# The last group of each feed-forward stage multiplied block by block instead of as seven products

## The chip, the cores and the metric

The kernel is one program on one core of a Trainium2 chip. The metric is device time in microseconds (us) of one execution; the profile shows one such execution in detail. TensorE is called PE (its weight loads PEld), VectorE DVE, ScalarE ACT, GpSimd POOL and SyncE SP.

## The reference

Two transformer-like blocks are applied to 512 tokens of width 1024, in float32: a first block (a convolution branch, two attentions, a merge, then a feed-forward stage) and a second one (attention, feed-forward, state-space layer, feed-forward). Only the three feed-forward stages matter here:

```python
# first block
h2 = rms_norm(x, g_mlp[l])
x = x + jnp.square(jax.nn.relu(h2 @ w_up[l])) @ w_down[l]      # 1024 -> 4096 -> 1024

# second block, after the attention (layer 0) and after the state-space layer (layer 1)
def conv_ffn(h, w_in, conv_w, conv_b, w_out):                  # 1024 -> 2 x 2816, 2816 -> 1024
    gate, up = jnp.split(h @ w_in, [D_FF_2], axis=-1)
    gate = causal_dwconv(gate, conv_w, conv_b)
    return (jax.nn.silu(gate) * up) @ w_out
```

The three stages come in this order: that of the first block, followed by the attention of the second block; `conv_ffn` layer 0, followed by the state-space layer; `conv_ffn` layer 1, after which the output is written.

## The kernel before

Activations and weights are split into a high part (float32 rounded to fp32r) and a low part (the remainder), and every product is three matmuls: high by high, high by low, low by high. ACT makes the high part by a cast, DVE the low part by a subtraction (`whi`, `wlo` for weights; `hh`/`hl`, `mhh`/`mhl`, `ffh`/`ffl`, `fsh`/`fsl` for features). All matmuls of a weight matrix are 128x128 by 128x512.

The whole kernel is a list of jobs, run one after the other by `run_jobs`. A job is a piece of a weight matrix; while one job's matmuls are issued, ACT and DVE split the weights of the next ones, up to nine chunks of 128x512 ahead, and generators (`spawn`) work on the results of earlier jobs. Which instruction stands before which on an engine is settled when the program is written, by a running estimate of each engine's time.

- `jobA` multiplies features by 256 columns of weights, features kept on the partitions of the result (banks `ga`). `jobB` and `projB` keep tokens on the partitions (banks `gb`): for each of four token tiles of 128 tokens they multiply by 512 columns. `projB` cuts the contraction into jobs of a few 128-row pieces (four, unless `cut` says otherwise) and holds four banks open between them. Their weights are loaded by SP into the two `raw` buffers, the next job's load being issued when the first chunk of this job is split.
- `Feat` holds split features: `put` casts and subtracts one 128x512 piece as soon as it is there, `rd` waits for it.
- `residual(half)` adds a bank to the residual stream `x` (two halves of 512 columns, four token tiles) and then calls `x_done`, which starts the sum of squares (`junk`), the transposes (`tr`) and the split of that piece for the next stage.

A feed-forward stage goes through its hidden features in groups: four of 1024 in the first block; 1024, 1024 and 768 in `conv_ffn`. A group's way down to 1024 columns is `seven`: its hidden features (512 tokens by 8 or 6 pieces of 128) and its rows of the weight matrix are each cut into 2 by 2 blocks, and the eight block products are replaced by seven products of sums of blocks (banks `gw`). The weight blocks are loaded by SP into the buffers `b` (`get`) and added up by POOL with accumulating DMAs (`add`). The hidden features stay whole in a `Hidden` object (`ffr`, `fsr`), and `operands` makes the left factor of each of the seven, in the order of the table SEVEN, each at most one product ahead of the one that PE is at (NOP): `11` and `12` are plain blocks, `s1`, `s4`, `s2`, `s3` are sums (in the profile `ffs`, `fss`, with `wt` between), `22` is a block again. After each product two pieces of `x` are updated by DVE.

The products of a group stand between the jobs of the next group's way up. The last group has no next group: its seven products stand alone, one behind the other, and `LASTS` says after which of them a piece of `x` is complete.

Of the kernel before, what the change touches and what calls it, by code (L numbers as in the profile page):

```python
# [21 lines left out]
KD = 8  # L22
# [49 lines left out]
def kernel(ctx: ExitStack, tc: tile.TileContext, ins: dict, out: bass.AP, parts=(1, 2, 3, 4, 5)):  # L72
# [481 lines left out]
    LASTS = {1: (0, 1), 4: (0, 0), 5: (1, 0), 6: (1, 1)}  # L554
    NOP = 2

# [75 lines left out]
    def seven(wap, r0, nk, H, scale, last, pre=None):  # L632
# [23 lines left out]
        def product(i):  # L656
            name, bk, new, (row, half, sign), over = SEVEN[i]

            def run(wt):
                quota[0] = 4  # L660
                if new:
                    for t in range(2):
                        banks[bk, t] = bank("g", "gw")
                order = [(k, t) for k in range(hk) for t in range(2)]
                by_token = last and i == 6
                if by_token:
                    order = [(k, t) for t in range(2) for k in range(hk)]

                def evac(t):
                    tt = 2 * row + t  # L670
                    xa = x_half(tt, half)
                    if over:
                        hand_over()
                    dve.scalar_tensor_tensor(out=xa, in0=banks[bk, t], scalar=scale(sign)[:, tt:tt + 1], in1=xa,
                                             op0=ALU.mult, op1=ALU.add)
                    if over:
                        rel("t")
                    if last and LASTS.get(i) == (row, half):
                        x_done(tt, half)

                for n, (k, t) in enumerate(order):
                    wh, wl = wt.get(k, 0, 512)
                    h, l = (x[:, t * 128:(t + 1) * 128] for x in H().at(name, k))
                    ps = banks[bk, t]
                    s, e = bool(new) and k == 0, k == hk - 1
                    pe.matmul(ps, lhsT=h, rhs=wh, start=s, stop=False, skip_group_check=True)
                    pe.matmul(ps, lhsT=h, rhs=wl, start=False, stop=False, skip_group_check=True)
                    pe.matmul(ps, lhsT=l, rhs=wh, start=False, stop=e, skip_group_check=True)
                    if by_token and e:
                        evac(t)  # L690
                    if n % 2 and n + 1 < len(order):
                        if not by_token:
                            wt.done()
                        yield
                H().done += 1
                if not by_token:
                    for t in range(2):
                        evac(t)
                yield

            return run
# [4 lines left out]
        for i in range(7):  # L706
            j = Job(None, hk, 512, product(i), pre if i == 0 else None)
            j.speed = 1.2
            j.source = lambda c, i=i: R[src[i]][:, c * 512:(c + 1) * 512]
            j.after = after[i]  # L710
            if i == 0:
                j.ahead = lambda: get("0", 1, 1)
                j.prefetch = lambda i: (get("2", 2, 1), get("1", 2, 2))
            out.append(j)
# [122 lines left out]
    def residual(c, last=True):  # L837

        def evac(tt, ps):
            xa = x_half(tt, c)  # L840
            dve.tensor_add(xa, ps, xa)
            if last:
                x_done(tt, c)
        return evac
# [4 lines left out]
    def first_block():  # L849
# [422 lines left out]
        def up_evac(g, k0):  # L1272
            def evac(ft, ps):
                if k0 + ft == 0:
                    F[g] = Hidden("ff", KD)
                F[g].half((k0 + ft) // 4)
# [3 lines left out]
                def rest():  # L1280
                    act.activation(out=F[g].slot(k0 + ft), in_=r, func=AF.Square)
                    F[g].got.add(("r", k0 + ft))
                    yield
# [8 lines left out]
        def down(g):  # L1292
            return seven(ins["w_down"], g * 1024, KD, lambda: F[g], lambda sign: G["by token"](sign, 2), g == 3,
                         (lambda: hooks.update(x=hooks["next1"])) if g == 3 else None)
# [3 lines left out]
        for g in range(4):  # L1298
            p = down(g)
            jobs.append(p[0])  # L1300
            if g == 3:
                jobs.extend(p[1:])
                break
            for i, ps in enumerate((p[1:3], p[3:5], p[5:7], ())):
                up(g + 1, i, (lambda g=g: F[g + 1].work()) if i == 3 else None)
                jobs.extend(ps)

# [211 lines left out]
    def conv_ffn(layer, G, nxt):  # L1519
# [17 lines left out]
        def up_evac(k0, g, base):  # L1537
            def evac(ft, ps):
                k = k0 + ft
                if k == base:  # L1540
                    F[g] = Hidden("fs", groups[g][1])
                until(lambda: k in gt)
                y = gt.pop(k)
                dve.tensor_mul(F[g].slot(k - base), ps, y)
                F[g].got.add(("r", k - base))
            return evac

        def down(g, base, nk, last):
            return seven(wo, base * 128, nk, lambda: F[g], lambda sign: G["by token"](sign, 1), last,
                         (lambda: hooks.update(x=hooks[nxt])) if last else None)  # L1550
# [4 lines left out]
        for g, (base, n) in enumerate(groups):  # L1555
            if p:
                jobs.append(p.pop(0))
            for i in range(n // 2):
# [4 lines left out]
                     pre=(lambda g=g: F[g].work()) if i == n // 2 - 1 else None)  # L1563
# [3 lines left out]
            p = down(g, base, n, g == 2)  # L1567
        jobs.extend(p)
# [424 lines left out]
```

## Time and profile before

| | |
|---|---|
| median of the runs | 2552.32 us (lowest 2549.96 us) |
| the profiled execution, its own time | 2547.46 us |
| its span in the trace | 2545.7 us |
| PE busy, PE weight loads busy | 97%, 78% of the span |
| DVE, ACT, POOL busy | 65%, 45%, 11% |
| TensorE clock granted, mean | 0.991 of full speed |

The span runs from the first to the last instruction of the profiled execution; its own time has 1.8 us around that. Matmuls overlap each other in the records (each is drawn 0.39 us long though the next starts 0.23 us later), so the distance from one start to the next is what a matmul costs.

### The profile page before, as it was taken

The numbers are of one execution on the slowest core, as the hardware profiler recorded it, in microseconds if no ns is written. First come the engines' busy times: TensorE is split into PE (matmuls) and PEld (weight loads), VectorE is DVE, ScalarE is ACT, GpSimd is POOL, SyncE is SP. The second block draws the span as 40 slices with busy tenths as digits, with TensorE's granted clock in tenths as the row PEclk, the third lists the DMA queues.
The fourth block names the chain that finished last, engine by engine and source line by source line (L and its number), as shares of the span: only waits on it lengthen the run. The fifth ranks groups of instructions, "written<-read, shape, count | busy, mean of one in ns | idle before, by whom it ended". The sixth has DMA issues, their size and how long they took to land.

```text
span 2545.7 us, 30879 instructions
## 1 busy us (share of the span) xinstructions
PE 2460.7 (97%) x11496; PEld 1977.5 (78%) x11496; DVE 1660.3 (65%) x3041; ACT 1154.7 (45%) x2451; POOL 290.4 (11%) x328
## 2 busy tenths in 40 slices
PE   8999999999999999989898999998999998999997
PEld 6777777788888888867676888885778886888886
DVE  6435679953444566676877566677688686667676
ACT  6445565632234444544555333334466535434333
POOL 1000111201110101122210000001011011001011
PEclk9999999999999999999999999999999998999999
DMA  5212222233233556642121354554333431245454
GB/s 203 100 66 89 94 67 68 68 126 103 90 135 114 131 137 156 149 83 85 34 100 34 113 136 116 132 122 83 107 96 89 120 112 58 89 143 116 133 112 107
DMA packets 213110, 268.45 MB, mean 105 GB/s; under 512 B 6976, under 2 KB 149696, under 8 KB 212960
## 3 DMA queue, kind: packets, MB, share of 16 engines
q1 hardware_dynamic: 189200, 220.21, 26.4%
q0 software_dynamic: 20736, 39.85, 9.8%
q10 hardware_dynamic: 3024, 6.42, 0.7%
q8 instruction: 90, 1.47, 0.2%
q14 instruction: 60, 0.49, 0.1%
HBM read 262.20 MB, written 4.26 MB: 105 GB/s over the span
## 4 chain that ended last, share of the span: by engine, by line
PE 87%; DVE 8%; ACT 1%; issue 1%; DMA 1%; POOL 1%; SPq 0%; ACTq 0%; DVEq 0%; POOLq 0%
PE ga L87 48%; PE gb L87 17%; PE gw L87 13%; PE y L87 2%; PE z L87 1%; DVE wlo L120 1%; PE as L87 1%; PE o L87 1%; PE aT L92 1%; DVE ae L120 1%; DVE x L120 1%; PE tr L92 1%; DVE sm L120 1%; DVE fy L120 1%; PE xs L87 1%
## 5 line engine op out<-in xcount | busy, mean ns | idle before, releaser
L87 PE MATMUL ga<-hh,whi 128*128 128x512 f32 x1672 | 668.9, 400 | 0.9 <-ACT hh L120 0.9
L87 PE MATMUL ga<-hh,wlo 128*128 128x512 f32 x1672 | 653.5, 391 | 0.3
L87 PE MATMUL ga<-hl,whi 128*128 128x512 f32 x1672 | 652.6, 390 | 1.0 <-DVE hl L120 1.0
L120 DVE TENSOR_TENSOR wlo<-raw,whi 128x512 fp32r<-128x512 f32 x661 | 454.8, 709 | 225.9 <-ACT whi L120 225.4
L120 ACT CAST whi<-raw 128x512 fp32r<-128x512 f32 x661 | 389.8, 616 | 134.8 <-PE ga L87 75.8
L87 PEld LDWEIGHTS ga<-hh,whi 128*128 128x128 f32 x1672 | 314.4, 188 | 70.1 <-issue 4.4
L87 PEld LDWEIGHTS ga<-hl,whi 128*128 128x128 f32 x1672 | 314.6, 188 | 68.0 <-issue 2.2
L87 PEld LDWEIGHTS ga<-hh,wlo 128*128 128x128 f32 x1672 | 314.0, 188 | 68.6 <-DVE wlo L120 1.1
L120 DVE TENSOR_TENSOR wlo<-b,whi 128x512 fp32r<-128x512 f32 x266 | 177.7, 685 | 40.9 <-ACT whi L120 40.6
L120 ACT CAST whi<-b 128x512 fp32r<-128x512 f32 x266 | 156.2, 616 | 60.1 <-DMA b<-in_ffn_w_out_dram 30.8
L87 PE MATMUL gb<-whi,hh 128*128 128x512 f32 (+1 forms) x416 | 169.9, 408 | 0.2 <-ACT hh L120 0.2
L120 DVE SCALAR_TENSOR_TENSOR x<-gw,rsp,x 128x512 f32<-128x512 f32 x140 | 100.2, 750 | 105.9 <-PE gw L87 105.7
L87 PE MATMUL gb<-whi,hl 128*128 128x512 f32 (+1 forms) x416 | 160.3, 385 | 1.3 <-DVE asc L120 1.3
L87 PE MATMUL gb<-wlo,hh 128*128 128x512 f32 (+1 forms) x416 | 159.7, 384 | 0.9 <-DVE wlo L120 0.9
L120 ACT ACTIVATE fy<-fy,cols 128x512 f32<-128x512 f32 x60 | 43.5, 725 | 211.5 <-DVE fy L120 211.5
L87 PE MATMUL gw<-whi,fss 128*128 128x512 f32 x352 | 115.9, 401 | 15.2 <-DVE fss L120 9.0
L652 POOL DMA_DIRECT2D b<-in_ffn_w_out_dram x48 | 55.5, 1238 | 610.6 <-DVE wlo L120 523.9
L120 DVE SCALAR_TENSOR_TENSOR fy<-fg,cols,fy 128x510 f32<-128x510 f32 (+1 forms) x136 | 102.8, 756 | 4.8
L120 DVE TENSOR_TENSOR fg<-ga,R 128x512 f32<-128x512 f32 x68 | 46.8, 689 | 82.4 <-PE ga L87 69.8
L87 PEld LDWEIGHTS gw<-whi,fss 128*128 128x128 f32 x352 | 66.9, 192 | 34.2 <-DVE fss L120 12.5
L87 PEld LDWEIGHTS gb<-whi,hl 128*128 128x128 f32 x416 | 78.9, 190 | 17.5 <-DVE hl L120 1.6
L87 PE MATMUL gw<-whi,ffs 128*128 128x512 f32 x256 | 83.0, 398 | 9.2 <-DVE ffs L120 7.9
(296 smaller groups left out, 4072.9 us busy)
## 6 DMA issues: line engine op xcount, KB each, us to landing
raw<-in_ffn_w_in_dram SPq DMA_DIRECT2D x44, 1024.0 KB, 5.1
raw<-in_w_in_dram SPq DMA_DIRECT2D x40, 1024.0 KB, 5.0
b<-in_ffn_w_out_dram POOLq DMA_DIRECT2D x40, 512.0 KB, 5.7
raw<-in_w_up_dram SPq DMA_DIRECT2D x16, 1024.0 KB, 5.4
b<-in_w_down_dram POOLq DMA_DIRECT2D x32, 512.0 KB, 6.0
raw<-in_ssm_w_in_dram SPq DMA_DIRECT2D x16, 1024.0 KB, 5.2
b<-in_w_down_dram SPq DMA_DIRECT2D x12, 1024.0 KB, 7.8
b<-in_ffn_w_out_dram SPq DMA_DIRECT2D x12, 1024.0 KB, 7.9
```

The lines of the kernel that those rows point to most:

```text
L87: nc.tensor.matmul(o, lhsT=lhsT, rhs=rhs, **kw)
L92: nc.tensor.transpose(o, i, idn)
L120: return fn(*args, **kw)
L652: nc.gpsimd.dma_start(out=r3(R[nm][:, a * 512:(c + 1) * 512], c + 1 - a), in_=dram(i, j, a, c + 1), accum_op=ALU.add)
```

## The change

`seven` loses the arguments for a last group; it now runs for all groups but the last. The last group's features go into a `Feat`, split piece by piece as they come, and its way down is two `projB` calls, one for each half of the 1024 columns: eight pieces of contraction in jobs of four and four in the first block, six pieces in jobs of two and four (`cut=[2, 4]`) in `conv_ffn`. `residual` takes a per-token scale and then does the update of `x` with `scaled_add`, the same instruction that `seven` uses. The last group has 1024 hidden features in the first block and 768 in `conv_ffn`.

```diff
-    LASTS = {1: (0, 1), 4: (0, 0), 5: (1, 0), 6: (1, 1)}
     NOP = 2
+
+    def scaled_add(ps, scale, tt, half):
+
+        xa = x_half(tt, half)
+        dve.scalar_tensor_tensor(out=xa, in0=ps, scalar=scale[:, tt:tt + 1], in1=xa, op0=ALU.mult, op1=ALU.add)
...
-    def seven(wap, r0, nk, H, scale, last, pre=None):
+    def seven(wap, r0, nk, H, scale):
...
-    def residual(c, last=True):
+    def residual(c, last=True, scale=None):
 
         def evac(tt, ps):
             xa = x_half(tt, c)
-            dve.tensor_add(xa, ps, xa)
+            if scale:
+                scaled_add(ps, scale(), tt, c)
+            else:
+                dve.tensor_add(xa, ps, xa)
             if last:
                 x_done(tt, c)
...
                 if k0 + ft == 0:
-                    F[g] = Hidden("ff", KD)
-                F[g].half((k0 + ft) // 4)
+                    F[g] = Hidden("ff", KD) if g < 3 else Feat("ff", KD)
+                if g < 3:
+                    F[g].half((k0 + ft) // 4)
...
                 def rest():
+                    if g == 3:
+                        act.activation(out=r, in_=r, func=AF.Square)
+                        yield from F[g].put(k0 + ft, r)
+                        return
...
-        for g in range(4):
+        for g in range(3):
             p = down(g)
             jobs.append(p[0])
-            if g == 3:
-                jobs.extend(p[1:])
-                break
             for i, ps in enumerate((p[1:3], p[3:5], p[5:7], ())):
-                up(g + 1, i, (lambda g=g: F[g + 1].work()) if i == 3 else None)
+                up(g + 1, i, (lambda g=g: F[g + 1].work()) if i == 3 and g < 2 else None)
                 jobs.extend(ps)
+        for half in range(2):
+            projB(ins["w_down"], 3 * 1024, KD, half * 512, lambda: F[3],
+                  residual(half, True, lambda: G["by token"](1, 2)),
+                  pre=(lambda: hooks.update(x=hooks["next1"])) if half == 0 else None)
...
-                    F[g] = Hidden("fs", groups[g][1])
+                    F[g] = Hidden("fs", 8) if g < 2 else Feat("fs", 8)
                 until(lambda: k in gt)
                 y = gt.pop(k)
+                if g == 2:
+                    dve.tensor_mul(y, ps, y)
+                    spawn(F[g].put(k - base, y), 0.9)
+                    return
...
-            p = down(g, base, n, g == 2)
-        jobs.extend(p)
+            p = []
+            if g < 2:
+                p = seven(wo, base * 128, n, lambda g=g: F[g], lambda sign: G["by token"](sign, 1))
+        for half in range(2):
+            projB(wo, 16 * 128, 6, half * 512, lambda: F[2], residual(half, True, lambda: G["by token"](1, 1)),
+                  cut=[2, 4], pre=(lambda: hooks.update(x=hooks[nxt])) if half == 0 else None)
```

Three places in the order of the instructions. On PE in the last group of the first block, as it was before, where the product `s1` begins (`gw` a bank, `ff` and `ffs` left factors of the seven, `x` a piece of the residual stream that is transposed into `tr`):

```order
L87 MATMUL gw<-whi_3_9217,ff_9147 128x512
L87 MATMUL gw<-whi_0_9230,ffs_9233 128x512
L87 MATMUL gw<-wlo_0_9231,ffs_9233 128x512
L87 MATMUL gw<-whi_0_9230,ffs_9233 128x512 x2
L87 MATMUL gw<-wlo_0_9231,ffs_9233 128x512
L87 MATMUL gw<-whi_0_9230,ffs_9233 128x512
L92 MATMUL tr<-ident,x_6506 128x128 x8
```

The same engine now, at the beginning of the last group, where the way up (`ga`) ends:

```order
L87 MATMUL ga<-hh_6805,wlo_3_9099 128x512
L87 MATMUL gb<-whi_0_9112,ffh_8631 128x512
L87 MATMUL gb<-wlo_0_9113,ffh_8631 128x512
L87 MATMUL gb<-whi_0_9112,ffl_8632 128x512
L87 MATMUL gb<-whi_1_9123,ffh_8631 128x512
L87 MATMUL gb<-wlo_1_9124,ffh_8631 128x512
L87 MATMUL gb<-whi_1_9123,ffl_8632 128x512
```

Before, each product of a sum needed a left factor made since the product before it; now each matmul reads features split during the way up. In all the last group has 192 such matmuls in place of 168 (first block), and 144 in place of 126 (each `conv_ffn`).

On DVE in the middle of the last group of the first block, before (`wt` and `ffs` belong to the left factors, `wlo` to the weights, `xg` and `hl` to the next stage's features):

```order
L120 TENSOR_TENSOR ffs_9233<-wt,ffs_9233 128x512
L120 SCALAR_TENSOR_TENSOR wt<-wt,ffr_8615 128x512
L120 SCALAR_TENSOR_TENSOR wt<-wt,ffr_8970 128x512
L120 TENSOR_TENSOR wlo_2_9330<-b_9100,whi_2_9329 128x512
L120 SCALAR_TENSOR_TENSOR x_6507<-gw,rsp,x_6507 128x512 x2
L120 TENSOR_TENSOR wlo_3_9345<-b_9100,whi_3_9344 128x512
L120 TENSOR_TENSOR hl_9311<-xg,hh_9310 128x4x128
L120 SCALAR_TENSOR_TENSOR wt<-wt,ffr_8615 128x512
L120 SCALAR_TENSOR_TENSOR wt<-wt,ffr_8970 128x512
L120 TENSOR_TENSOR hl_9311<-xg,hh_9310 128x4x128
L120 TENSOR_TENSOR ffs_9333<-wt,ffs_9333 128x512
```

And now, between the two halves of the columns:

```order
L120 SCALAR_TENSOR_TENSOR x_6506<-gb,rsp,x_6506 128x512
L120 TENSOR_TENSOR wlo_2_9292<-raw_9170,whi_2_9291 128x512
L120 TENSOR_TENSOR xg<-tr,cols 128x512
L120 TENSOR_TENSOR hl_9300<-xg,hh_9299 128x4x128
L120 SCALAR_TENSOR_TENSOR x_6507<-gb,rsp,x_6507 128x512
L120 TENSOR_TENSOR wlo_3_9321<-raw_9170,whi_3_9320 128x512
L120 TENSOR_TENSOR wlo_0_9344<-raw_9245,whi_0_9343 128x512
```

The left factors are gone from the queue; what is left are the low parts of the weights, the updates of `x` and the next stage's features.

On PE at the end of the last group of `conv_ffn` layer 0, before, where the state-space layer's first job begins (`ga`):

```order
L87 MATMUL gw<-whi_2_15103,fs_15138 128x512
L87 MATMUL gw<-wlo_2_15104,fs_15138 128x512
L87 MATMUL gw<-whi_2_15103,fs_15138 128x512
L92 MATMUL tr<-ident,x_6507 128x128 x8
L87 MATMUL ga<-hh_15080,whi_0_15116 128x512
L87 MATMUL ga<-hl_15081,whi_0_15116 128x512
```

And now:

```order
L92 MATMUL tr<-ident,x_6507 128x128 x4
L87 MATMUL gb<-whi_2_14899,fsh_14705 128x512
L87 MATMUL gb<-wlo_2_14900,fsh_14705 128x512
L87 MATMUL gb<-whi_2_14899,fsl_14706 128x512
L87 MATMUL gb<-whi_3_14935,fsh_14705 128x512
L87 MATMUL gb<-wlo_3_14936,fsh_14705 128x512
L87 MATMUL gb<-whi_3_14935,fsl_14706 128x512
L87 MATMUL ga<-hh_14857,whi_0_14964 128x512
```

Before, all eight last transposes stood in one row ahead of the first `ga`; now four stand six matmuls earlier and the last four stand behind twelve `ga`. Outside the last groups the order of PE is nearly unchanged: 14 of 878 rows differ in the second block's attention, none in the state-space layer.

## Rows read from the trace of the kernel before

**Rows 1.** The page: busy time, share of the span and instructions of each engine

```profile
PE 2460.7 (97%) x11496; PEld 1977.5 (78%) x11496; DVE 1660.3 (65%) x3041; ACT 1154.7 (45%) x2451; POOL 290.4 (11%) x328
```

**Rows 2.** Stretches: length, busy PE, PEld, DVE, ACT, POOL, clock, DMA

```profile
755.33:802.22 46.89, 46.89 (x222) 38.78 (x220) 23.68 (x39) 16.97 (x36) 2.71 (x3) 1.00 0.37 127
1092.62:1151.18 58.56, 46.13 (x197) 34.78 (x196) 43.62 (x71) 28.65 (x58) 11.81 (x8) 0.97 0.39 62
1719.62:1785.20 65.58, 53.37 (x215) 39.57 (x214) 46.50 (x85) 27.88 (x60) 11.01 (x10) 0.92 0.39 80
2500.36:2541.10 40.74, 32.33 (x127) 23.91 (x125) 29.88 (x51) 12.55 (x25) 6.41 (x6) 0.96 0.54 106
```

**Rows 3.** Longest waits of PE in its second, third, fourth stretch: total, times, longest

```profile
PE gw L87 <- DVE ffs L120: 7.9, 5, 3.6
PE gw L87 <- DVE ff L120: 2.8, 2, 1.7
...
PE gw L87 <- DVE fss L120: 4.5, 3, 2.5
PE gw L87 <- ACT fss L120: 2.6, 3, 1.1
...
PE gw L87 <- DVE fss L120: 4.5, 3, 1.8
PE gw L87 <- ACT fss L120: 3.6, 2, 2.7
```

**Rows 4.** Timeline of PE in the first block's last group: start, length, instruction

```profile
1117.09 0.73 PE L87 MATMUL gw<-whi,ffs 128*128 128x512 f32 x2 [3.63 <-DVE ffs L120]
...
1118.03 1.05 PE L87 MATMUL gw<-whi,ffs 128*128 128x512 f32 x2
...
1119.31 1.05 PE L87 MATMUL gw<-whi,ffs 128*128 128x512 f32 x2
```

**Rows 5.** Timeline of DVE during that wait

```profile
1114.42 1.41 DVE L120 SCALAR_TENSOR_TENSOR wt<-wt,ffr 128x512 f32<-128x512 f32 x2
1115.75 0.68 DVE L120 TENSOR_TENSOR hl<-xg,hh 128x512 fp32r<-128x512 f32 x1
1116.35 0.68 DVE L120 TENSOR_TENSOR ffs<-wt,ffs 128x512 fp32r<-128x512 f32 x1
```

**Rows 6.** Timeline of PE through the first block's w_out: two `projB`, then `ga`

```profile
755.33 0.39 PE L87 MATMUL gb<-whi,mhh 128*128 128x512 f32 x1
...
769.16 0.39 PE L87 MATMUL gb<-wlo,mhh 128*128 128x512 f32 x1
...
793.98 0.60 PE L92 MATMUL tr<-ident,x 128*128 128x128 f32 x4
...
797.18 0.60 PE L92 MATMUL tr<-ident,x 128*128 128x128 f32 x4
...
802.22 0.39 PE L87 MATMUL ga<-hh,whi 128*128 128x512 f32 x1
```

**Rows 7.** Timeline of PE around conv_ffn layer 0's last group and the state-space layer's start

```profile
1714.18 0.39 PE L87 MATMUL gw<-whi,fs 128*128 128x512 f32 x1
...
1770.34 0.50 PE L87 MATMUL ga<-hh,whi 128*128 128x512 f32 x1 [0.91 <-ACT hh L120]
...
1785.20 0.39 PE L87 MATMUL ga<-hh,whi 128*32 128x512 f32 x1
```

**Rows 8.** Timeline of PE where conv_ffn layer 0 begins, after the attention's `jobB`

```profile
1402.21 0.40 PE L87 MATMUL ga<-hh,whi 128*128 128x512 f32 x1
...
1411.72 0.48 PE L87 MATMUL ga<-hh,whi 128*128 128x512 f32 x1
```

**Rows 9.** DMA issues: kind, count, KB each, us from issue to landing

```profile
raw<-in_w_up_dram SPq DMA_DIRECT2D x16, 1024.0 KB, 5.4
...
out_dram<-x SPq DMA_DIRECT2D x4, 512.0 KB, 2.7
```

**Rows 10.** Timeline of DVE: its last instruction

```profile
2541.14 0.75 DVE L120 SCALAR_TENSOR_TENSOR x<-gw,rsp,x 128x512 f32<-128x512 f32 x1 [1.29 <-PE gw L87]
```

More of the change, by code (lines that the diff above doesn't have):

```diff
@@ L663, in run @@
                         banks[bk, t] = bank("g", "gw")
[L664 to L669, printed above, removed]
+                for k in range(hk):
+                    wh, wl = wt.get(k, 0, 512)
+                    for t in range(2):
+                        h, l = (x[:, t * 128:(t + 1) * 128] for x in H().at(name, k))
+                        ps = banks[bk, t]
+                        pe.matmul(ps, lhsT=h, rhs=wh, start=bool(new) and k == 0, stop=False, skip_group_check=True)
+                        pe.matmul(ps, lhsT=h, rhs=wl, start=False, stop=False, skip_group_check=True)
+                        pe.matmul(ps, lhsT=l, rhs=wh, start=False, stop=k == hk - 1, skip_group_check=True)
+                    if k + 1 < hk:
+                        wt.done()
+                        yield
@@ L670, in evac @@
+                H().done += 1
+                for t in range(2):
                     tt = 2 * row + t
-                    xa = x_half(tt, half)
                     if over:
                         hand_over()
-                    dve.scalar_tensor_tensor(out=xa, in0=banks[bk, t], scalar=scale(sign)[:, tt:tt + 1], in1=xa,
-                                             op0=ALU.mult, op1=ALU.add)
+                    scaled_add(banks[bk, t], scale(sign), tt, half)
                     if over:
@@ L677, in evac @@
                         rel("t")
[L678 to L698, printed above, removed]
                 yield
@@ L706, in seven @@
         for i in range(7):
-            j = Job(None, hk, 512, product(i), pre if i == 0 else None)
+            j = Job(None, hk, 512, product(i))
             j.speed = 1.2
@@ L1292, in down @@
         def down(g):
-            return seven(ins["w_down"], g * 1024, KD, lambda: F[g], lambda sign: G["by token"](sign, 2), g == 3,
-                         (lambda: hooks.update(x=hooks["next1"])) if g == 3 else None)
+            return seven(ins["w_down"], g * 1024, KD, lambda: F[g], lambda sign: G["by token"](sign, 2))
         for i in range(4):
             up(0, i, (lambda: F[0].work()) if i == 3 else None)
-        for g in range(4):
+        for g in range(3):
             p = down(g)
             jobs.append(p[0])
-            if g == 3:
-                jobs.extend(p[1:])
-                break
             for i, ps in enumerate((p[1:3], p[3:5], p[5:7], ())):
-                up(g + 1, i, (lambda g=g: F[g + 1].work()) if i == 3 else None)
+                up(g + 1, i, (lambda g=g: F[g + 1].work()) if i == 3 and g < 2 else None)
                 jobs.extend(ps)
+        for half in range(2):
+            projB(ins["w_down"], 3 * 1024, KD, half * 512, lambda: F[3],
+                  residual(half, True, lambda: G["by token"](1, 2)),
+                  pre=(lambda: hooks.update(x=hooks["next1"])) if half == 0 else None)
     def attn(G):
@@ L1546, in up_evac @@
             return evac
-        def down(g, base, nk, last):
-            return seven(wo, base * 128, nk, lambda: F[g], lambda sign: G["by token"](sign, 1), last,
-                         (lambda: hooks.update(x=hooks[nxt])) if last else None)
         groups = ((0, 8), (8, 8), (16, 6))
@@ L1562, in conv_ffn @@
                 jobA(w, FF2 + k0 * 128, X, up_evac(k0, g, base),
-                     pre=(lambda g=g: F[g].work()) if i == n // 2 - 1 else None)
+                     pre=(lambda g=g: F[g].work()) if i == n // 2 - 1 and g < 2 else None)
                 jobs.extend(p[1:2])
```

## The prediction

> **What bounds the kernel now.** Read the table of engines first: PE is busy 97% of the span, so it sets the time, and DVE (65%) and ACT (45%) matter only where PE waits for them [rows 1]. A change that adds matmuls to such a kernel looks like a loss, so the next question is where the missing 3% lie. For that I cut the trace into stretches. Three of them are the last groups of the three feed-forward stages; the fourth, for comparison, is the product with w_out in the first block, which is done by two `projB` calls over eight pieces of contraction, with `residual` and `x_done` behind, as the changed last group will be; it is the first row of [rows 2]. There PE is busy for 46.89 of 46.89 us at a clock of 1.00. In the last groups it is busy for 46.13 of 58.56, 53.37 of 65.58 and 32.33 of 40.74 us, at a mean clock of 0.97, 0.92 and 0.96 [rows 2]. (The first stretch runs from the first matmul of the group to the first of the attention; the second begins 24 matmuls after the first row of [rows 7] and is drawn on to 1785.20 us, into the state-space layer, since PE stumbles there too; the third ends with PE's last matmul.)
>
> Then the list of waits in these stretches: PE waits for `ffs`, `ff`, `fss`, the left factors of the seven products, made by ACT and DVE; the two longest entries of each are together 25.9 us [rows 3]. The timeline shows one of them from close by: PE stands for 3.63 us until DVE has made `ffs` [rows 4], and DVE, in those microseconds, works off a queue of two sums `wt`, a low part of the next stage's features, and only then the factor [rows 5]. After that wait three matmuls take 1.28 us (1118.03 to 1119.31), where three usually take 0.68: PE runs at the lower of its two clock levels (1.2 instead of 2.4 GHz) for a while after having stood [rows 4]. In the middle groups such factors are made while the next group's way up runs; the last group has nothing to run meanwhile.
>
> **The price of a matmul.** In the w_out product 61 matmuls start between 755.33 and 769.16 us, so one costs 0.2267 us. Twelve matmuls with one group of four transposes take 3.20 us (793.98 to 797.18), so the group costs 0.48 us. Check: 192 matmuls and 7 groups are 43.53 + 3.36 = 46.89 us, and the stretch is 46.89 us long (755.33 to 802.22) [rows 2, 6]: in this form of work PE loses nothing.
>
> A page of the Trainium skill, "TensorE: Matmul & The Clock Gate", section "Back-to-back issue gap", gives N / 2.4 + 2.5 ns for an isolated matmul, 215.7 ns at 512 columns, and about 131 ns for a sustained stream. By these the 60 matmuls that the change adds would cost 12.9 or 7.9 us. The rows show 226.7 ns and decide.
>
> **The change, part by part.**
>
> *Matmuls.* A last group of eight pieces is 2 halves x 4 token tiles x 8 pieces x 3 = 192 matmuls instead of 7 x 4 x 2 x 3 = 168; one of six pieces is 144 instead of 126. Together 24 + 18 + 18 = 60 more, x 0.2267 = 13.6 us, all on PE and so all on the path.
>
> *Lost time.* What do the last groups cost beyond their matmuls? First block: 168 x 0.2267 + 7 x 0.48 = 41.45 us of 58.56, so 17.1 us lost. Layer 0 of conv_ffn: 126 x 0.2267 + 7 x 0.48 = 31.92 us, and then what the state-space layer does until 1785.20. That part is 36 matmuls, a group of transposes, the eight matmuls of `R`, and 12 more matmuls; the same row of work, without a wait, stands at the start of conv_ffn layer 0, where its first three parts take 9.51 us (1402.21 to 1411.72) [rows 8]; with 12 x 0.2267 = 2.72 it is 12.23 us. So 44.15 of 65.58, 21.4 us lost, some of it behind 1770.34, where `ga` first waits for `hh` [rows 7]. Layer 1: 126 x 0.2267 = 28.56 of 40.74 us (nothing is transposed at the end of the program), 12.2 us lost. In all 50.7 us.
>
> *What becomes of it.* Bounds: all of it can stay, or all of it can go. The nearest row is the w_out product, same helper, same tile shapes, same work behind each bank, with no loss at all; I take that value. Why it should hold: the features of the last group are split while its way up still runs (one more cast and one subtraction per piece); the first projB job of 24 or 48 matmuls (5.4 or 10.9 us) uses the earliest pieces and gives the last ones time. DVE and ACT lose the sums and seven sets of factors, and split 16 or 12 weight chunks in place of 28 or 21. DVE's load in the w_out stretch is 23.68 us of 46.89, in the last group of the first block it is 43.62 of 58.56 [rows 2]. What hides the weight splits is a job's 10.9 us of matmuls; were that cover gone, each chunk would show.
>
> *Transfers.* The three block loads of a last group and its accumulating DMAs on POOL go; four `raw` loads on SP come (1 MB each in the first block; 0.5 and 1 MB in turn in `conv_ffn`). They wait for a `raw` buffer, and behind them on SP stand the next stage's weight loads. 1 MB lands 5.4 us after its issue [rows 9], against 10.9 us of matmuls per job of four pieces: hidden, 0 us. Were it not, a load would cost up to 5.4 us.
>
> *Boundaries.* At the attention's start the order is as before (one group of transposes after 12 of its matmuls); 0 us. At the state-space layer's start the transposes now stand spread among matmuls, as they do in [rows 8]; that gain is in the sum. At the end the last update of `x` starts at 2541.14 and the span ends at 2545.7 us [rows 10]; the output leaves in four transfers of 2.7 us each [rows 9], now 12 matmuls or 2.72 us apart. Between 0 and 2.7 us (one transfer standing behind another); I take 0.
>
> *Sum.* First block: 46.89 instead of 58.56, 11.7 us less. Layer 0: 32.64 + 3.36 + 12.23 = 48.23 instead of 65.58, 17.4 less. Layer 1: 32.64 instead of 40.74, 8.1 less. Together 37.1 us, that is 50.7 regained less 13.6 added. The profiled execution of 2547.46 us would become 2510.3 us (a span of 2508.6). The median of the runs lies 4.9 us and the lowest 2.5 us above that execution, so measured runs should come out at 2513 to 2515; I say 2514, 1.5% less than before.
>
> **The rivals.**
>
> *Some waits come back.* The first matmuls on the last features could wait for their split, since a last piece passes through DVE and ACT several times. For it: DVE still carries weights and `x`. Against it: those features are wanted 5 to 11 us after the group begins. Price: one wait like the longest (3.63 us) in each group, and at least six matmuls behind it slowed by 0.2 us, 4.8 us each, 14.5 in all: 2530.
>
> *Late loads: slower than before.* The seven products read weights loaded well ahead; the `projB` jobs depend on two `raw` buffers, the next load being issued when the first chunk of this job is split, and in `conv_ffn` a job of two pieces lasts only 5.4 us. If each of the twelve loads showed in full, that is 12 x 5.4 = 64.8 us against 37.1 us gained: 2580. It decides from 3.1 us per load on. Against it: the stretch of w_out has the same loads and no loss [rows 2, 6], and chunks are split up to nine ahead.
>
> *More matmuls on the busiest engine, and nothing back.* If the losses belong to DVE's other work at these places (weights, `x`, next features), they stay, and the 13.6 us are simply added: 2566. Against it: the waits name the factors [rows 3]. The Trainium skill's page "Perfetto Trace Analysis", section "Identifying the Most-Contended Engine", says to find the most occupied engine and to improve that one first, which speaks against giving PE more work. The same section says that matmul busy time is a bad measure of headroom, and that the weight loads' share is better; in the stretches [rows 2] that share is 83% in the w_out product and 59 to 60% in the last groups, so the trace agrees with the second half.
>
> That the change does not do what it says is excluded by the order of its instructions.
>
> **How the numbers follow.** Forecast as summed 0.86; some waits 0.10; late loads 0.02; nothing back 0.02. The range goes from 2506 (the sum by the profiled execution, and some 4 us as runs differ) to 2526 (two of the three waits of the first rival back). More than 2% is about what a measurement of this kernel can tell from no change; it is 51 us here, as much as all the lost time without the added matmuls. So faster by over 2% gets 0.03, slower by over 2% 0.01, for what no case here names, and within 2% 0.96.
>
> **What would show it.** In the trace of the changed kernel the first block's last group should last 46.9 us from its first `gb` to the attention, with 192 matmuls 0.227 us apart and no wait; those of `conv_ffn` 36.0 and 32.6 us; the clock there 1.00; the stretch from the state-space layer's first `ga` to its first 32-column matmul 12.2 us instead of 14.9 (1770.34 to 1785.20). Waits for `ffh`, `fsh`, `fsl` or `whi` behind a `raw` load in these stretches would prove me wrong, as would waits that turn up in the attention or at the end.

## The result, and the profile after

The changed kernel takes 2508.07 us (median of 4 runs, 2507.32 to 2509.19) against 2551.74 us before (2549.96 us the lowest) on the same chip: the ratio is 0.9832, 95% interval 0.9812 to 0.9851, so 38 to 48 us less. By the bound of 2% that is no clear change; the interval says that it is faster. One of the four executions of the kernel before took 5217.33 us and counts in its median; without it that is 2551.15 us. The forecast was 2514 us. The profiled execution took 2507.32 us with a span of 2505.6 us; 2510.3 and 2508.6 had been forecast.

First the page of the changed kernel, busy time of each engine; it answers to [rows 1]:

```profile
span 2505.6 us, 30744 instructions
...
PE 2456.9 (98%) x11556; PEld 1984.7 (79%) x11556; DVE 1608.5 (64%) x2947; ACT 1129.9 (45%) x2399; POOL 259.4 (10%) x304
```

PE has 60 matmuls more, as worked out, and the span is 40.1 us shorter. Its busy time falls by 3.8 us in spite of them, and so does that of the three last groups (131.8 us in the last three of [rows 2], 128.0 us below): before, their fewer matmuls ran in part at the lower clock level (0.97, 0.92 and 0.96 on the mean, 1.00 now) and were drawn longer.

The stretches of the three last groups, cut at the same instructions as in [rows 2] (the second one to the state-space layer's first 32-column matmul); columns: length, busy PE, PEld, DVE, ACT, POOL, clock, DMA share, GB/s:

```profile
1092.92:1139.81 46.89, 46.89 (x221) 38.78 (x220) 23.31 (x38) 18.44 (x39) 1.11 (x2) 1.00 0.25 77
1705.80:1754.14 48.34, 48.34 (x234) 39.92 (x233) 28.96 (x52) 18.28 (x41) 2.59 (x4) 1.00 0.30 90
2468.43:2501.23 32.80, 32.80 (x145) 26.84 (x143) 11.61 (x18) 2.90 (x6) 0.00 (x0) 1.00 0.22 78
```

PE is busy through all of them, at a clock of 1.00 instead of 0.97, 0.92 and 0.96. They were to last 46.89, 48.23 and 32.64 us. DVE's work in the first one falls from 43.62 to 23.31 us.

The cuts, in the timeline of PE:

```profile
1092.92 0.39 PE L87 MATMUL gb<-whi,ffh 128*128 128x512 f32 x1
...
1139.81 0.28 PE L87 MATMUL gb<-whi,hh 128*128 128x256 f32 x1
...
1705.80 0.39 PE L87 MATMUL gb<-whi,fsh 128*128 128x512 f32 x1
...
1741.81 0.40 PE L87 MATMUL ga<-hh,whi 128*128 128x512 f32 x1
...
1754.14 0.39 PE L87 MATMUL ga<-hh,whi 128*32 128x512 f32 x1
```

From the state-space layer's first `ga` to its first 32-column matmul it is 12.33 us (14.86 before [rows 7]; 12.2 forecast).

PE's longest waits in the whole program (what waits, for whom, total, times, longest):

```profile
PE as L87 <- POOL qz L120: 6.7, 5, 2.2
PE y L87 <- DVE m L120: 5.4, 3, 3.0
PE tr L92 <- DMA memt<-in_mem_dram: 4.0, 1, 4.0
PE gb L87 <- DVE oTl L120: 3.8, 2, 2.8
PE gb L87 <- ACT whi L120: 3.4, 2, 3.1
```

The waits for `ffs`, `ff` and `fss` of [rows 3] are gone, and none of what is left lies in the three stretches: the wait for `whi` is elsewhere, and no `ffh`, `fsh` or `fsl` is waited for.

Where the 40.1 us of the span come from, piece by piece, each the same two instructions in both traces:

| from, to | before | after | difference |
|---|---|---|---|
| start to the first block's last group | 1092.62 | 1092.92 | +0.3 |
| first block's last group | 58.56 | 46.89 | −11.7 |
| attention, to the first `R` of `conv_ffn` layer 0 | 259.7 | 257.3 | −2.4 |
| to that layer's last group | 308.7 | 308.7 | 0.0 |
| last group and start of the state-space layer | 65.58 | 48.34 | −17.2 |
| to layer 1's last group | 715.2 | 714.3 | −0.9 |
| last group of layer 1 | 40.74 | 32.80 | −7.9 |
| to the end | 4.6 | 4.4 | −0.2 |

The forecast for these rows was −11.7, −17.4, −8.1 and 0 elsewhere. Only the attention differs by more than 1 us, and it gains its time in its first 28.8 us. That stretch in the windows of the kernel before:

```profile
1151.18:1180.00 28.82, 27.24 (x164) 24.55 (x163) 16.11 (x45) 12.34 (x28) 4.67 (x6) 0.94 0.35 115
```

PE's waits in it:

```profile
PE gb L87 <- DVE asc L120: 1.3, 1, 1.3
PE gb L87 <- ACT hh L120: 0.2, 1, 0.2
```

The windows of the changed kernel, from the same matmul on:

```profile
1139.81:1168.63 28.82, 28.82 (x179) 25.81 (x178) 15.68 (x46) 12.51 (x27) 5.53 (x7) 1.00 0.33 114
```

PE has no wait there, and in the same 28.82 us it now has 15 matmuls more: there too waits (1.5 us in all) and a lower clock had belonged to what the old last group left undone. The first two experiments below bear this out. In the state-space layer I had looked behind the border of the stage, here not.

By the attention's first matmul into a bank `as` 3.5 us are gained (38.65 us instead of 42.14). A net 1.0 us is lost again behind a wait for `qz`, here in the changed kernel and then in the one of the first experiment, which has the same order of instructions there:

```profile
1247.06 0.89 PE L87 MATMUL as<-kbT,qz 128*128 128x256 f32 x2 [2.24 <-POOL qz L120]
```

```profile
1248.73 0.70 PE L87 MATMUL as<-kbT,qz 128*128 128x256 f32 x2 [2.23 <-POOL qz L120]
```

The granted clock fell to 0.5 behind the first and stayed at 1.00 behind the second, whose attention is 3.6 us shorter than before (256.1 us instead of 259.7). So the change is worth some 3.5 us there, and 1.0 of it is missing from this execution by its clock.

At the end, DVE's last update of `x`; it answers to [rows 10], and the tail of the program behind it did not grow, though 0 to 2.7 us had been left open:

```profile
2501.27 0.75 DVE L120 SCALAR_TENSOR_TENSOR x<-gb,rsp,x 128x512 f32<-128x512 f32 x1 [1.97 <-PE gb L87]
```

### The profile page after: what moved, and what is told of

It is laid out like the page before. It is cut to its first block, busy times and chain, and to the rows that moved or that the text cites. A ratio compares the mean times of both kernels' runs of the same rounds, so it can differ in the third digit from the quotient of the medians.

```text
span 2505.6 us, 30744 instructions
## 1 busy us (share of the span) xinstructions
PE 2456.9 (98%) x11556; PEld 1984.7 (79%) x11556; DVE 1608.5 (64%) x2947; ACT 1129.9 (45%) x2399; POOL 259.4 (10%) x304
## 4 chain that ended last, share of the span: by engine, by line
PE 90%; DVE 6%; ACT 1%; issue 1%; DMA 1%; POOL 1%; SPq 0%; ACTq 0%; DVEq 0%; POOLq 0%
PE ga L87 49%; PE gb L87 21%; PE gw L87 11%; PE y L87 2%; PE z L87 1%; PE as L87 1%; PE tr L92 1%; PE o L87 1%; DVE wlo L120 1%; PE aT L92 1%; DVE ae L120 1%; DVE fy L120 1%; PE xs L87 1%; PE xo L87 1%; DVE sm L120 1%
## 5 line engine op out<-in xcount | busy, mean ns | idle before, releaser
L120 DVE TENSOR_TENSOR wlo<-raw,whi 128x512 fp32r<-128x512 f32 x701 | 481.5, 708 | 234.9 <-ACT whi L120 234.4
L120 ACT CAST whi<-raw 128x512 fp32r<-128x512 f32 x701 | 411.9, 616 | 145.0 <-PE ga L87 63.2
L120 DVE TENSOR_TENSOR wlo<-b,whi 128x512 fp32r<-128x512 f32 x196 | 131.2, 686 | 36.8 <-ACT whi L120 36.8
L120 ACT CAST whi<-b 128x512 fp32r<-128x512 f32 x196 | 114.1, 615 | 15.5 <-PE gw L87 11.2
L120 DVE SCALAR_TENSOR_TENSOR x<-gw,rsp,x 128x512 f32<-128x512 f32 x98 | 70.0, 750 | 69.3 <-PE gw L87 69.2
L656 POOL DMA_DIRECT2D b<-in_ffn_w_out_dram x32 | 38.5, 1202 | 507.7 <-DVE wlo L120 503.8
L87 PEld LDWEIGHTS gb<-wlo,hh 128*128 128x128 f32 x416 | 78.7, 189 | 14.4 <-DVE wlo L120 0.8
L87 PEld LDWEIGHTS gb<-whi,hh 128*128 128x128 f32 x416 | 78.5, 189 | 14.1 <-issue 1.0
L87 PE MATMUL gw<-whi,fss 128*128 128x512 f32 x256 | 81.4, 389 | 0.0
```

The costliest lines, as they stand in the source:

```text
L87: nc.tensor.matmul(o, lhsT=lhsT, rhs=rhs, **kw)
L120: return fn(*args, **kw)
L656: nc.gpsimd.dma_start(out=r3(R[nm][:, a * 512:(c + 1) * 512], c + 1 - a), in_=dram(i, j, a, c + 1), accum_op=ALU.add)
```

## The experiments

The theory: the seven products of a last group stood alone, so that ACT and DVE could not make the left factors in time; multiplied by blocks, the last group reads features that were split during its own way up, and each added matmul costs 0.227 us. The rivals: the late factors could be a matter of how far ahead they are made, of the work at a stage's end that shares DVE with them, or the block form could simply be the better form everywhere. All times below are medians; the kernel before took 2550.7, 2549.6 and 2548.5 us beside the three sets of runs.

**One stage at a time.** The kernel before with the change's parts in the first block alone (`conv_ffn` as before):

```diff
-        for g in range(4):
+        for g in range(3):
...
+        for half in range(2):
+            projB(ins["w_down"], 3 * 1024, KD, half * 512, lambda: F[3],
```

And the other way round, `conv_ffn` alone:

```diff
-                    F[g] = Hidden("fs", groups[g][1])
+                    F[g] = Hidden("fs", 8) if g < 2 else Feat("fs", 8)
...
+        for half in range(2):
+            projB(wo, 16 * 128, 6, half * 512, lambda: F[2], residual(half, True, lambda: G["by token"](1, 1)),
```

> Only the first block's last group is multiplied block by block; both conv_ffn stages keep seven products. Theory (each last group loses its own time to waits for left factors, and gives it back by itself): that group 47 us instead of 58.6, the attention behind it about 2.4 us shorter as in the changed kernel, so about 14 us less than before, 2536 to 2539. Rival (the gain comes from less load on DVE, ACT and the DMA queues in the whole kernel): the parts do not add up, and this one gives clearly less or more than a third of the 44 us.

> Only the two conv_ffn stages are changed; the first block keeps seven products in all groups. Theory: 17.4 us and 8.1 us less, together 25 to 30 us less than before, 2522 to 2527, and with the first part alone the sum of both is the whole change. Rival (load in the whole kernel): the two parts do not add up to the 44 us.

Measured: 2536.1 us (2534.6 to 2536.9; ratio 0.9941, 0.9926 to 0.9956) and 2526.75 us (2525.0 to 2527.7; 0.9905, 0.9889 to 0.9922): 14.6 and 24.0 us less. Both times lie in the theory's ranges; the second gain is 1 us short of the 25 to 30 us that were named. PE's waits for left factors with the first block alone changed:

```profile
PE gw L87 <- DVE fss L120: 8.8, 6, 2.5
...
PE gw L87 <- ACT fss L120: 6.3, 5, 2.7
```

Their 15.1 us are those of `conv_ffn`'s two entries in [rows 3] (15.2). With `conv_ffn` alone changed, the first block's stay:

```profile
PE gw L87 <- DVE ffs L120: 7.8, 5, 3.6
...
PE gw L87 <- DVE ff L120: 2.8, 2, 1.7
```

So each stage's waits go with that stage's change. The attention's start goes with the first block: from its first matmul to the first one into a bank `as` it is 38.64 us in the first kernel and 42.14 in the second, against 42.14 before and 38.65 after. The two gains together are 38.6 us, 4 short of the whole change's 42.6 (2550.7 to 2508.07). The traces place this gap outside the edits. The stretches that were changed last what they last in the changed kernel: 46.89 us for the first block's group, 48.56 and 32.81 us for the other two (48.34 and 32.80 after). But the first block's last group begins 1.7 and 0.9 us later, and the unchanged stretch from the state-space layer's first 32-column matmul to layer 1's last group takes 716.9 and 717.5 us instead of 714.3. So the parts add up where they were edited, and the rival of a lighter load in the whole kernel is not needed.

**Blocks in every group.** All ten groups by `projB`, no seven products at all:

```diff
-        for g in range(3):
-            p = down(g)
...
+        for g in range(4):
+            for i in range(4):
+                up(g, i)
+            for half in range(2):
+                projB(ins["w_down"], g * 1024, KD, half * 512, lambda g=g: F[g],
+                      residual(half, g == 3, lambda: G["by token"](1, 2)),
```

> Every group of the three stages is multiplied block by block, no seven products are left: 7 more groups of eight pieces, 7 x 24 = 168 matmuls more than in the changed kernel. Theory (in the middle groups the left factors are made under the next group's way up and cost PE nothing): 168 x 0.2267 = 38 us more than the changed kernel, 2546, no new waits. Rival (seven products cost more than their matmuls wherever they are, so blocks are the better form): no slower than the changed kernel, 2508 or less.

Measured: 2545.9 us (10 runs, 2543.3 to 2547.6; 0.9979, 0.9970 to 0.9988), 37.8 us more than the changed kernel. Its page:

```profile
PE 2492.4 (98%) x11724; PEld 2016.5 (79%) x11724; DVE 1471.0 (58%) x2719; ACT 1069.1 (42%) x2273; POOL 191.5 (8%) x248
```

168 matmuls more than after, by 0.2267 us, are 38.1 us. So the added matmuls account for the whole difference, the middle groups had nothing to give back, and the block form is not better in itself.

**Left factors made earlier.** The kernel before, each left factor up to two products ahead instead of one:

```diff
-    NOP = 2
+    NOP = 3
```

> The kernel before, with the left factors allowed two products ahead of PE instead of one (NOP = 3). Theory A (the waits come from factors that are begun too late): most of the 50.7 us of lost time goes and none of the matmuls is added, 2502 to 2520, faster than the changed kernel or near it. Theory B (DVE and ACT have too much to do in these stretches whatever the order): the waits only move, 2540 to 2555.

Measured: 2540.9 us (2538.6 to 2542.1; 0.9960, 0.9945 to 0.9974), 9.8 us less. PE's waits on the seven products:

```profile
PE gw L87 <- DVE x L120: 4.9, 8, 2.1
...
PE gw L87 <- DVE ffs L120: 4.8, 3, 1.8
PE gw L87 <- DVE fsr L120: 4.0, 1, 4.0
...
PE gw L87 <- DVE fss L120: 3.0, 2, 2.2
PE gw L87 <- ACT fss L120: 2.6, 1, 2.6
```

The waits for the factors shrink, and others take their place: for the updates of `x` that free the banks, and for a sum of `fsr`. A lead of one more product buys a quarter of what the change does. In the trace 3.3 us of it are in the first block's last group (55.27 instead of 58.56), 3.6 in the attention's start (38.58 us instead of 42.14) and 2.7 in layer 1's last group; layer 0's stretch is no shorter. A still longer lead was not tried, so what it would buy is open.

**A middle group without its cover.** The changed kernel, but the seven products of the first block's third group stand alone, as the last group's once did; the instructions are the same, only their order differs:

```diff
-            jobs.append(p[0])
-            for i, ps in enumerate((p[1:3], p[3:5], p[5:7], ())):
+            alone = g == 2
+            jobs.extend(p if alone else p[0:1])
+            for i, ps in enumerate(((),) * 4 if alone else (p[1:3], p[3:5], p[5:7], ())):
```

> The changed kernel, but in the first block the third group's seven products stand alone, one behind the other, ahead of the fourth group's way up, and not between its jobs. The same instructions, no matmul more or less. Theory (seven products lose time wherever nothing else runs between them): 10 to 17 us more than the changed kernel, 2518 to 2525, as waits for ffs and ff. Rival (what delays the left factors is the work for the next stage at a stage's end, transposes and the features hl, of which a middle group has none): at most 4 us more, 2508 to 2512.

Measured: 2519.7 us (2518.8 to 2521.3; 0.9880, 0.9863 to 0.9896), 11.6 us more than the changed kernel. One of three waits for `ffs` (5.7 us in all), in the timeline of PE:

```profile
1033.37 1.05 PE L87 MATMUL gw<-whi,ffs 128*128 128x512 f32 x2 [2.42 <-DVE ffs L120]
1034.21 0.63 PE L87 MATMUL gw<-wlo,ffs 128*128 128x512 f32 x1
1034.64 1.06 PE L87 MATMUL gw<-whi,ffs 128*128 128x512 f32 x2
1035.49 0.63 PE L87 MATMUL gw<-wlo,ffs 128*128 128x512 f32 x1
```

It has the look of [rows 4]: a wait for a sum, then three matmuls in 1.27 us (1033.37 to 1034.64), the lower clock level. The stretch from the last matmul that both kernels have in the same place to the last group's first, the same 336 instructions in another order, in this kernel and then in the changed one:

```profile
1016.84:1103.38 86.54, 80.00 (x338) 63.87 (x337) 51.52 (x81) 38.35 (x69) 7.22 (x6) 0.98 0.41 92
```

```profile
1016.01:1092.92 76.91, 76.65 (x339) 63.17 (x337) 51.41 (x81) 38.02 (x69) 7.22 (x6) 1.00 0.46 105
```

That is 9.6 us; the rest lies in stretches that no edit touches (0.8 us ahead of this one and 1.9 from the state-space layer's first 32-column matmul to layer 1's last group). Here no stage ends, so the missing cover alone costs some 10 of the 17.1 us that the first block's old last group lost. The work at the stage's end may be the other 7; that is the difference of two kernels and not a run of its own. The Trainium skill's page "Perfetto Trace Analysis", section "Optimization Strategy", says that where the most-contended engine changes over time, interleaving such stretches may help. This pair of runs shows a gain of that kind and prices it, though PE stays the busiest engine even while the seven products stand alone (36.62 of 43.16 us from 1016.84 on, DVE 34.40).

**Last features first.** The changed kernel, but each `projB` of a last group begins with the pieces that were made last:

```diff
-            projB(ins["w_down"], 3 * 1024, KD, half * 512, lambda: F[3],
+            projR(ins["w_down"], 3 * 1024, half * 512, lambda: F[3],
...
+                  ((4, 4), (0, 4)),
```

> The changed kernel with the order of the pieces turned round: each half of the columns begins with the features that were made last (pieces 4 to 7 in the first block, 4 and 5 in conv_ffn). Theory (the first job on early features is what hides the split of the last ones): in the first block PE waits for about two ACT steps, a cast and a subtraction of 0.6 to 0.7 us each and what stands ahead of them, 2.5 to 5 us; in conv_ffn a product of 5.4 us stands between, so 0 to 1 us each; 2510 to 2515 against 2508 of the changed kernel. Rival (the features are ready in any order): 2508, no wait.

Measured: 2510.3 us (2509.0 to 2511.4; 0.9842, 0.9828 to 0.9857), and no wait of 2.5 us. The only one in the group, in the timeline of PE:

```profile
1096.72 0.50 PE L87 MATMUL gb<-whi,ffh 128*128 128x512 f32 x1 [0.34 <-ACT ffh L120]
```

The group takes 47.80 us instead of 46.89; those of `conv_ffn` are unchanged (48.34 and 32.80 us). The trace is longer by 1.3 us ahead of the group and by 1.0 us in the state-space layer too, where nothing was edited. So the median lies at the edge of the theory's range, but its waits are not there: the features are ready almost as soon as the way up ends, and that early pieces come first is worth at most 0.9 us, not a condition of the gain.

**Short jobs.** The changed kernel with all jobs of the last groups cut to two pieces, so twice as many right-factor loads of half the size:

```diff
-                  residual(half, True, lambda: G["by token"](1, 2)),
+                  residual(half, True, lambda: G["by token"](1, 2)), cut=[2, 2, 2, 2],
...
-                  cut=[2, 4], pre=(lambda: hooks.update(x=hooks[nxt])) if half == 0 else None)
+                  cut=[2, 2, 2], pre=(lambda: hooks.update(x=hooks[nxt])) if half == 0 else None)
```

> The changed kernel with all projB jobs of the last groups cut to two pieces: 20 loads of 0.5 MB in place of 12 of 0.5 or 1 MB, each issued only 5.4 us of matmuls ahead or less. Theory (loads are hidden by the nine chunks split ahead): no change, 2506 to 2511. Rival (loads through two buffers are just hidden): one microsecond or more per load shows, 2520 or more, as waits of PE for whi of these loads.

Measured: 2514.6 us (2512.7 to 2516.3; 0.9859, 0.9844 to 0.9874), 6.5 us more than the changed kernel: neither side's number. No `whi` is waited for in the last groups. What is new is at the attention's start, in the timeline of PE:

```profile
1145.20 0.38 PE L87 MATMUL gb<-whi,hl 128*128 128x256 f32 x1 [2.47 <-DVE hl L120]
...
1145.91 0.41 PE L87 MATMUL gb<-wlo,hh 128*128 128x256 f32 x1
1146.12 0.42 PE L87 MATMUL gb<-whi,hl 128*128 128x256 f32 x1
1146.34 0.41 PE L87 MATMUL gb<-whi,hh 128*128 128x256 f32 x1
```

A wait for the next stage's left factor, and behind it matmuls of 256 columns 0.21 us apart instead of 0.12. My reading was that the last job is to blame: its matmuls are what stands between two updates of `x`. Two runs were to tell this from the loads. The first has short jobs and a long last one (`conv_ffn` stays at `[2, 4]`):

```diff
-                  residual(half, True, lambda: G["by token"](1, 2)),
+                  residual(half, True, lambda: G["by token"](1, 2)), cut=[2, 2, 4],
```

The second is the reverse:

```diff
-                  residual(half, True, lambda: G["by token"](1, 2)),
+                  residual(half, True, lambda: G["by token"](1, 2)), cut=[4, 2, 2],
...
-                  cut=[2, 4], pre=(lambda: hooks.update(x=hooks[nxt])) if half == 0 else None)
+                  cut=[4, 2], pre=(lambda: hooks.update(x=hooks[nxt])) if half == 0 else None)
```

> The changed kernel with the first block's last group in jobs of 2, 2 and 4 output pieces (the other two last groups as before). If the run with all jobs of two pieces lost its 6.5 us because its last job was short, so that the residual updates came close together and the next stage's first left factors late, then here the last job is long again, TensorE waits for no hl at the attention's start, and the time is that of the changed kernel: 2507 to 2509 us. If the right factors' loads, twice as many and half as large, were the cause, about half to two thirds of the loss stays: 2511 to 2513 us, with waits for whi or a later start of the attention.

> The changed kernel with the jobs of the first block's last group cut into 4, 2 and 2 output pieces, and the convolution block's last groups into 4 and 2. If the short last job is the cause, the wait of some 2.5 us for hl at the attention's start and the slow matmuls behind it are back, and the time is 2512 to 2516 us, nearly that of the run with all jobs of two pieces. If the loads or the first job's length were the cause, the time is that of the changed kernel, 2507 to 2509 us.

Measured: 2510.1 us (2507.9 to 2510.7; 0.9844, 0.9827 to 0.9861) and 2514.2 us (2512.2 to 2515.1; 0.9861, 0.9847 to 0.9876). The first median lies between the two numbers that had been named for it, so the traces have to decide. DVE's last four updates of `x` in the kernel with the long last job:

```profile
1131.64 0.75 DVE L120 SCALAR_TENSOR_TENSOR x<-gb,rsp,x 128x512 f32<-128x512 f32 x1 [7.99 <-PE gb L87]
1134.83 0.75 DVE L120 SCALAR_TENSOR_TENSOR x<-gb,rsp,x 128x512 f32<-128x512 f32 x1 [0.70 <-PE gb L87]
1138.02 0.75 DVE L120 SCALAR_TENSOR_TENSOR x<-gb,rsp,x 128x512 f32<-128x512 f32 x1
1141.28 0.74 DVE L120 SCALAR_TENSOR_TENSOR x<-gb,rsp,x 128x512 f32<-128x512 f32 x1
```

And in the kernel with the short one:

```profile
1136.81 0.75 DVE L120 SCALAR_TENSOR_TENSOR x<-gb,rsp,x 128x512 f32<-128x512 f32 x1 [5.05 <-PE gb L87]
1138.18 0.75 DVE L120 SCALAR_TENSOR_TENSOR x<-gb,rsp,x 128x512 f32<-128x512 f32 x1 [0.61 <-PE gb L87]
1140.08 0.74 DVE L120 SCALAR_TENSOR_TENSOR x<-gb,rsp,x 128x512 f32<-128x512 f32 x1
1141.82 0.75 DVE L120 SCALAR_TENSOR_TENSOR x<-gb,rsp,x 128x512 f32<-128x512 f32 x1 [0.17 <-PE gb L87]
```

In that kernel PE then has this wait:

```profile
1146.86 0.38 PE L87 MATMUL gb<-whi,hl 128*128 128x256 f32 x1 [2.47 <-DVE hl L120]
```

Four updates lie 3.2 us apart with twelve matmuls between them and 1.4 to 1.9 us apart with six. In the short case the last pieces come too close together for their transposes and splits, and the attention waits for `hl`. From the attention's first matmul to its first into `as` the windows give, for the long last job:

```profile
1141.04:1179.67 38.63, 37.20 (x219) 32.53 (x217) 21.10 (x59) 17.80 (x36) 11.60 (x11) 1.00 0.33 111
```

And for the short one:

```profile
1141.98:1183.54 41.56, 37.59 (x222) 32.65 (x220) 22.73 (x61) 18.59 (x39) 12.51 (x12) 1.00 0.29 99
```

That is 2.9 us for the first block's short last job; the changed kernel takes 38.65 us, the one with all jobs short 43.05 us. At the state-space layer's start, group included, the long last job takes 48.31 us (as after), the short one 49.44 us. Together 4.0 us, and the two medians differ by 4.1. Both kernels have the same loads, two more of `w_down` than the changed kernel; only the order of the jobs differs. So the length of the last job is the cause, and two loads more are not. The eight loads of the kernel with all jobs short were not tried with a long last job. That the kernel with the long last job lies 2.1 us above the changed kernel comes from elsewhere: its last group starts at 1094.14 instead of 1092.92, behind the same order of matmuls, the unchanged stretch up to layer 1's last group takes 1.1 us longer, and group and attention's start last as long as after.

## Why the prediction was right

*What bounds the kernel.* Right: PE sets the time, and what it lost stood in the last groups and just behind them. The first two experiments place the waits in them stage by stage.

*The price of a matmul.* 0.2267 us held: 46.89 us forecast and measured for 192 matmuls and 7 groups of transposes, and 37.8 us for the 168 matmuls of the kernel in blocks against 38.1.

*The lost time.* All but 0.3 of the 50.7 us came back, where I had put the nearest row, the w_out product, between all and nothing: the three stretches are 36.8 us shorter (37.1 forecast). Layer 0's and layer 1's groups lie 0.1 and 0.2 us over the sum; no run shows why.

*Why it should hold.* Two reasons were given. The one, that the features are split during the way up, holds. The other, that the first job uses the earliest pieces and gives the last ones time, was over-sized: with the last pieces first the group is 0.9 us longer.

*Transfers at 0.* Right: no wait for `whi` in the three stretches, not even with loads of half the size. The loads of `w_down` land 4.9 us after their issue (the median), inside jobs of 10.9 us.

*Boundaries.* The attention's start, taken as 0, gave 3.5 us, of which the attention as a whole kept 2.4: a mis-sized term. The order of its instructions was right (the first difference stands 88 instructions of PE in, and the time is gained before it), but a wait for `asc` and a lower clock behind the old group went too. Such waits had been named as a sign of being wrong if they turned up anew, not as lost time that the attention already had. The state-space layer's start (12.33 us against 12.2) and the end (0) were right.

*From the sum to the runs.* The profiled execution came out 3.0 us below the forecast: 2.4 from the attention, 0.9 from the stretch before layer 1's last group, the rest in the small terms. The median lies 6 us below, since I added 3 to 5 us for the distance between the profiled execution of before and its other runs, while the changed kernel's profiled execution lies only 0.75 us below its median. That distance was too long by some 1 us: the median of 2552.32 us that it was taken from had three executions, one of them of 5217.33 us.

*The rivals.* Waits that come back: none did, and the run that provoked them has one of 0.34 us. Late loads and nothing back: excluded by the stretches. The Trainium skill's page "Perfetto Trace Analysis", section "Identifying the Most-Contended Engine", was read as speaking against more work for PE; it says only to optimize the busiest engine first, and with 60 matmuls more on that engine the kernel is faster, so the reading failed. Its second half is borne out: the weight loads' share in the last groups, which the page calls a better measure than matmul busy time, rises from 59 to 60% to 82 or 83% (38.78 of 46.89 us, 26.84 of 32.80).

## What to carry to other kernels

A form with fewer matmuls and more preparation pays only where other work covers the preparation: here seven products win 38 us in the groups that are interleaved, and in those that stand alone they cost 12, 17 and 8 us more than blocks, so the form belongs to the place and not to the kernel. Price such a swap from a stretch of the same trace that already works in the other form, and look for lost time behind the stage's border too, where late features slow the start of the next one. When the contraction is cut into jobs, let the last one be long: it spaces the results that the next stage starts from.

## What was not expected of the hardware

A wait of the same length was not always followed by the lower clock. PE stood 2.47 us for `hl` at the same place in two kernels. With all jobs short, matmuls of 256 columns were 0.21 us apart from 0.7 us after it until about 1149.2, and the stretch to the first `as` has a granted clock of 0.96:

```profile
1140.32:1183.37 43.05, 39.08 (x221) 34.15 (x220) 22.84 (x61) 18.48 (x39) 12.50 (x12) 0.96 0.29 95
```

With only the last jobs short they stayed 0.12 us apart, and the clock was 1.00:

```profile
1147.55 0.28 PE L87 MATMUL gb<-wlo,hh 128*128 128x256 f32 x1
1147.67 0.28 PE L87 MATMUL gb<-whi,hl 128*128 128x256 f32 x1
1147.79 0.28 PE L87 MATMUL gb<-whi,hh 128*128 128x256 f32 x1
```

In both PE had been busy up to the wait, with the same attention matmuls and transposes just before it. The same stretch took 43.05 us in the one and 41.56 us in the other, so a wait's cost can't be read from its length alone.

Executions differ by 1 to 2.4 us where nothing was changed: the first block's last group starts at 1092.92 us in the changed kernel and at 1095.27 us in the one with long jobs first, behind the same order of PE's instructions. Of these 2.35 us 1.6 arise at one place, near 118 us: behind the same two waits (0.82 and 1.02 us) the latter's matmuls run 0.43 us apart for a while, the former's 0.23. The unchanged stretch from the state-space layer's first 32-column matmul to layer 1's last group took 714.3 to 717.5 us in the ten traces that have it in the same form. The last groups themselves, which are without a wait in the changed kernel, repeat within 0.1 us (46.89, 46.89 and 46.90 us in three kernels that share that group). So a few us between medians of four runs decide little here, and a trace cut at the same instructions decides more.
